# A two-layer hybrid decoder step: VectorE, ScalarE and GpSimd in program order

## Chip, cores and metric

One core of one Trainium2 chip. The metric is the device time of one launch in microseconds, as the median of several runs.

## The reference

One inference step of a decoder with two layers, d = 1024, on 544 tokens: a prompt of 512 and 8 samples of 4 tokens, which share the weights. Cut to what matters, per layer:

```
h  = rmsnorm(x) * (1 + scale1(c)) + shift1(c)
z  = h @ W_in                       # all mixers' inputs and the merge gates
A  = causal pooling (windows 2, 4, 8, 16), a linear map per group
B  = retention, 4 heads, rotary q and k, chunks of 128, group norm, swish gate
C  = B_ * conv3(C_ * h_)            # short gated convolution
D  = RWKV-7: token shift, decay, delta-rule state S = S*w + (S a) b + v k, gate
mixed = sum over branches of sigmoid(gate_i) * (branch_i @ W_i)
x  = x + gate1(c) * (mixed @ W_out)
h2 = rmsnorm(x) * (1 + scale2(c)) + shift2(c)
u  = causal_dwconv3(h2 @ W_up);  x = x + gate2(c) * ((silu(u_a) * u_b) @ W_down)
```

After the second layer a final RMSNorm. The new states of every mixer are outputs too. All data is fp32.

## The kernel before

**Matmuls.** Channels lie on the 128 partitions and tokens in the free dimension, in two halves of 272 columns. A product of fp32 accuracy is made of three matmuls (`mm3`: hi of the weight times hi and lo of the input, lo of the weight times hi of the input; L137, L138, L139, and L164, L165, L166 after the change). A weight unit is 128x1024: a DMA on SyncE's queue brings it as `raw` (three buffers), ScalarE makes `whi` by a CAST (L117), VectorE, and in two cases GpSimd, makes `wlo`, the residual (L118). A unit gives 24 matmuls per half into a PSUM bank `pd` (three buffers). Small matmuls go to `pm` (five buffers).

**Main stream and generators.** `tile_hybrid_step` emits the main stream (first steps of the input projection by `first_units` together with the modulation's products, the rest of the projection, `gates` four times, out-projection, FFN up and down, norm), and after every three matmuls it calls `slot()`, which lets generators (`spawn`) go a step if they are due: `rwkv` with its scan, `retentions`, the norms, the modulation's weights. A `yield n` in a generator says after how many matmuls the next step is due. So each piece of side work has its place among the matmuls.

**Who sets the order.** The tile framework schedules. TensorE is under `manual_schedule`: its instructions run in the order in which the program emits them. For the other engines a scheduler with a simulated timeline sets the order (`schedule_with_timeline_sim=True`), and `tc.high_priority()` moves a few evacuations ahead:

```
with tile.TileContext(nc, schedule_with_timeline_sim=True) as tc:
    with tc.manual_schedule(engines={mybir.EngineType.PE}):
```

**Names and lines that come up below.** `evac_rw` evacuates a unit of RWKV's input (ScalarE L1008 copy, L1009 scaled copy; VectorE L1013 adds the token shift). `products(T)` makes the decays and key products of a chunk (ScalarE L467, L468; VectorE L477, L479, L485, L491), which L510 multiplies. `substitute` solves a triangular system in 31 steps on VectorE and GpSimd, before the scan. The scan (`psG`, `gs` L625, matmul L630) has gaps of D_G, D_S and D_P matmuls between its steps. `gates` makes a sigmoid per unit-half (ScalarE L1140), the branch's product, times the sigmoid (VectorE L1122) and the sum (VectorE or GpSimd L1124). RWKV's last stage is VectorE L782 to L786 and a split into hi (ScalarE L398) and lo (VectorE L399). In `retention`, L803 to L813 are the transposes' copies and masks, L835 to L842 the chunk states (L836, L838 on VectorE, used by the matmul L855), L871 to L877 the outputs' copies and squares, L387 the group norm's matmul with L392 and L395 on ScalarE (a square root, or a logarithm or exponential, each with a table load). `residual` adds a projection to x (VectorE L350, for the samples L354, L357), `sum_sq` squares (ScalarE L280) and adds (VectorE L283), `rstd_of` sums by a matmul (L291), takes a root (L293) and a reciprocal (L294); `norm_half` multiplies (L313), `modulate` scales and shifts (ScalarE L301, samples on VectorE L304, L305), and splits (L398, L399).

Of the kernel before, what the change touches and what calls it, by code (L numbers as in the profile page):

```python
# [25 lines left out]
D_G, D_S, D_P = 16, 16, 20  # L26
# [17 lines left out]
def tile_hybrid_step(ctx: ExitStack, tc: tile.TileContext, io: dict):  # L44
# [63 lines left out]
    def load_unit(l, u):  # L108
        raw = wp.tile([128, 1024], F32, tag="raw", name=nm("raw"), bufs=3)
        nc.sync.dma_start(raw, io["wst"][l, u])  # L110
        dst = extra_pools.get((l, u))
# [5 lines left out]
        S.copy(hi, raw)  # L117
        (G if (l, u) in ((0, 1), (0, 2)) else V).tensor_tensor(out=lo, in0=raw, in1=hi, op=SUB)  # L118
        wloaded[(l, u)] = (hi, lo)

    order = [(l, u) for l in range(L) for u in range(NU)]
    wpos = [0]

    def prefetch(l, u, ahead):
        while wpos[0] < len(order) and wpos[0] <= l * NU + u + ahead:
            load_unit(*order[wpos[0]])
            wpos[0] += 1

    def getw(l, u, ahead=3):
        prefetch(l, u, ahead)  # L130
        return wloaded[(l, u)]
# [16 lines left out]
    nmm, gens = [0], []  # L148
# [15 lines left out]
    def slot():  # L164
        for e in [e for e in gens if not e["pe"] and nmm[0] >= e["due"]]:  # L165
# [111 lines left out]
    def sum_sq(acc, x):  # L277
# [5 lines left out]
        V.tensor_tensor(out=acc, in0=acc, in1=sq, op=ADD)  # L283
        return acc

    def rstd_of(accs):

        out = []
        for acc in accs:
            ps = PM()  # L290
            PE.matmul(ps[:, 0:HALF], lhsT=ones, rhs=acc, start=True, stop=True)  # L291
            rs = ZR(HALF)
            S.activation(rs, ps[:, 0:HALF], AF.Sqrt, bias=EPS6)  # L293
            V.reciprocal(rs, rs)  # L294
            out.append(rs)
        return out

    def modulate(u, k, half, sA, shA, hh):
        c0, c1 = HS[half]
        npc = HALF if half == 0 else SEQ - HALF  # L300
        S.activation(u[:, :npc], u[:, :npc], AF.Identity, bias=shA[:, k, 0:1], scale=sA[:, k, 0:1])  # L301
        if half == 1:
            us = smp(u[:, npc:HALF])
# [93 lines left out]
    def split_hilo(src, hi, lo):  # L397
        S.copy(hi, src)  # L398
        V.tensor_tensor(out=lo, in0=src, in1=hi, op=SUB)  # L399

    def rwkv(l, za, zb, M, yD):
# [51 lines left out]
        def products(T):  # L453
# [41 lines left out]
        bkn = products(0)  # L495
        yield 60, True
        for T in range(5):
# [3 lines left out]
            if T < 4:  # L501
                bkn = products(T + 1)
# [30 lines left out]
            if T < 4:  # L533
                yield 56, True
# [1045 lines left out]
```

## Time and profile before

| | |
|---|---|
| runs | 1990.83, 1991.24, 1987.48 us; median 1990.83 |
| profiled execution | 1989.65 us, its span 1987.9 us |
| mean granted TensorE clock | 0.984 |
| busy: TensorE matmul | 1916.1 us, 96% |
| busy: weight load | 1837.4 us, 92% |
| busy: VectorE | 1099.3 us, 55% |
| busy: ScalarE | 837.2 us, 42% |
| busy: GpSimd | 330.0 us, 17% |

One execution was profiled. PE is TensorE's matmul, PEld its weight load (it overlaps), DVE VectorE, ACT ScalarE, POOL GpSimd, SP SyncE. L12 is line 12 of the kernel. Times are us from the span's start unless marked ns. In a table of stretches each engine has its busy time and count, PEclk is the TensorE clock that the throttle granted (1.00 is full speed). In a list of waits a row names who waited, for whom, the total, the number of waits and the longest. In a timeline a row has its start, its length, the instruction, and in brackets the idle time before it with what ended it.

### The profile page before, as it was taken

Reading aid. Unit: us, or ns where it says so; the run is one execution under the profiler, and the core shown is the slowest. Engines: PE = TensorE matmul, PEld = TensorE weight load, DVE = VectorE, ACT = ScalarE, POOL = GpSimd, SP = SyncE. Lnnn points to the kernel's source line nnn. Section 1 sums busy time; section 2 is a strip of 40 time slices with the busy share of each in tenths; the row PEclk is TensorE's granted clock in tenths of the full one; section 3 lists DMA queues with packets and bytes.
Section 4 is the critical chain, followed back from the end, with each engine's and each line's share of the span. In section 5 each row is a group of like instructions: output and inputs, shape, how many; then the busy total and the mean of one; then the engine's idle time right before and its main releaser. Section 6 shows DMA issues by size and latency. Waiting matters only on the chain.

```text
span 1987.9 us, 39257 instructions
## 1 busy us (share of the span) xinstructions
PE 1916.1 (96%) x16188; PEld 1837.4 (92%) x16188; DVE 1099.3 (55%) x2245; ACT 837.2 (42%) x1585; POOL 330.0 (17%) x655
## 2 busy tenths in 40 slices
PE   5999999999999999999999999999999999999997
PEld 4989998889999998899999899989899999999997
DVE  5476655443565643456673766554435766455565
ACT  4643233263345531435355433334523555243542
POOL 2210024213001210102202101342210012011210
PEclk8999999999999999999999999999999999999999
DMA  8223434512433257622332133233124222222231
GB/s 319 87 86 99 139 118 151 171 58 85 133 114 136 86 205 292 233 86 85 126 123 65 65 86 86 67 122 102 58 88 162 72 75 89 93 86 86 89 100 47
DMA packets 75555, 227.16 MB, mean 114 GB/s; under 512 B 20208, under 2 KB 23072, under 8 KB 73584
## 3 DMA queue, kind: packets, MB, share of 16 engines
q1 hardware_dynamic: 69872, 210.43, 31.7%
q0 software_dynamic: 3536, 11.53, 1.7%
q10 hardware_dynamic: 1968, 2.69, 0.5%
q8 instruction: 127, 2.08, 0.4%
q14 instruction: 52, 0.43, 0.1%
HBM read 213.33 MB, written 9.06 MB: 112 GB/s over the span
## 4 chain that ended last, share of the span: by engine, by line
PE 87%; DVE 5%; ACT 3%; DMA 2%; issue 2%; SPq 0%; ACTq 0%; DVEq 0%; POOL 0%; POOLq 0%
PE pd L137 27%; PE pd L139 26%; PE pd L138 26%; PE pm L240 2%; DVE wlo L118 1%; DMA raw<-in_wst 1%; PE pm L663 1%; PE pm L683 1%; DVE z L617 1%; PE pm L687 1%; DMA t<-in_xinit 0%; DMA t<-in_wada 0%; PE pm L510 0%; DVE t L953 0%; PE pm L517 0%
## 5 line engine op out<-in xcount | busy, mean ns | idle before, releaser
L137 PE MATMUL pd<-t,whi 128*128 128x272 f32 x4104 | 1211.3, 295 | 21.1 <-ACT t L398 9.6
L138 PE MATMUL pd<-t,whi 128*128 128x272 f32 x4104 | 1186.2, 289 | 5.7 <-DVE t L399 5.7
L139 PE MATMUL pd<-t,wlo 128*128 128x272 f32 x4104 | 1191.0, 290 | 0.0
L137 PEld LDWEIGHTS pd<-t,whi 128*128 128x128 f32 x4104 | 777.5, 189 | 56.6 <-issue 23.8
L138 PEld LDWEIGHTS pd<-t,whi 128*128 128x128 f32 x4104 | 779.4, 190 | 7.8 <-DVE t L399 6.5
L139 PEld LDWEIGHTS pd<-t,wlo 128*128 128x128 f32 x4104 | 778.3, 190 | 0.0
L118 DVE TENSOR_TENSOR wlo<-raw,whi 128x1024 fp32r<-128x1024 f32 x256 | 315.3, 1232 | 318.6 <-ACT whi L117 318.0
L117 ACT CAST whi<-raw 128x1024 fp32r<-128x1024 f32 x258 | 270.5, 1049 | 447.0 <-PE pd L138 425.0
L1287 POOL COPY off<-zr 128x18 f32<-128x18 f32 x88 | 77.2, 877 | 572.4 <-ACT zr L1285 572.4
L350 DVE SCALAR_TENSOR_TENSOR t<-pd,mod,t 128x272 f32<-128x272 f32 (+1 forms) x160 | 76.5, 479 | 115.2 <-PE pd L139 115.0
L1285 ACT COPY zr<-pd 128x272 f32<-128x272 f32 (+2 forms) x264 | 72.9, 311 | 85.4 <-PE pd L139 85.4
L1140 ACT ACTIVATE zr<-pd 128x272 f32<-128x272 f32 x128 | 50.6, 396 | 123.4 <-PE pd L139 122.9
L1124 POOL TENSOR_TENSOR t<-t,zr 128x272 f32<-128x272 f32 x64 | 73.6, 1168 | 144.6 <-DVE zr L1122 106.4
L1122 DVE TENSOR_TENSOR zr<-pd,zr 128x272 f32<-128x272 f32 x96 | 40.5, 435 | 90.3 <-PE pd L139 89.9
L1051 DVE SCALAR_TENSOR_TENSOR zr<-zr,par,zr 128x560 f32<-128x560 f32 x92 | 73.4, 801 | 6.6 <-ACT zr L1050 6.6
L1052 DVE SCALAR_TENSOR_TENSOR zr<-zr,par,zr 128x560 f32<-128x560 f32 x92 | 73.6, 801 | 2.7
L1050 ACT ACTIVATE zr<-zr,par 128x560 f32<-128x560 f32 x92 | 70.0, 764 | 7.0
L399 DVE TENSOR_TENSOR t<-zr,t 128x544 fp32r<-128x544 f32 (+1 forms) x96 | 54.2, 578 | 29.2 <-ACT t L398 29.2
L280 ACT ACTIVATE zr<-t 128x272 f32<-128x272 f32 (+1 forms) x72 | 31.9, 454 | 88.4 <-DVE t L350 62.1
L398 ACT CAST t<-zr 128x544 fp32r<-128x544 f32 (+1 forms) x96 | 48.8, 530 | 47.7 <-DVE zr L1298 46.7
L139 PE MATMUL pd<-t,t 128*128 128x272 f32 x224 | 64.7, 289 | 0.0
L137 PE MATMUL pd<-t,t 128*128 128x272 f32 x224 | 64.5, 288 | 0.0
(283 smaller groups left out, 1777.4 us busy)
## 6 DMA issues: line engine op xcount, KB each, us to landing
raw<-in_wst SPq DMA_DIRECT2D x276, 512.0 KB, 3.4
t<-in_wada SPq DMA_DIRECT2D x32, 1024.0 KB, 9.2
raw<-in_wada SPq DMA_DIRECT2D x24, 512.0 KB, 3.5
zr<-in_rope POOLq DMA_DIRECT2D x16, 272.0 KB, 3.8
t<-in_wada SPq DMA_DIRECT2D x8, 512.0 KB, 6.9
t<-in_xT SPq DMA_DIRECT2D x4, 544.0 KB, 6.4
zr<-zr ACTq DMA_DIRECT2D x32, 68.0 KB, 3.2
t<-in_xT SPq DMA_DIRECT2D x2, 1088.0 KB, 8.5
```

The source lines that it names most:

```text
L117: S.copy(hi, raw)
L118: (G if (l, u) in ((0, 1), (0, 2)) else V).tensor_tensor(out=lo, in0=raw, in1=hi, op=SUB)
L137: PE.matmul(ps, lhsT=a, rhs=xh, start=first, stop=False)
L138: PE.matmul(ps, lhsT=a, rhs=xl, start=False, stop=False)
L139: PE.matmul(ps, lhsT=b, rhs=xh, start=False, stop=last)
L350: V.scalar_tensor_tensor(out=x[:, c0:c0 + npc], in0=ps[:, :npc], scalar=gate[:, m, 0:1], in1=x[:, c0:c0 + npc], op0=MUL, op1=ADD)
L1050: S.activation(cv, u[:, 0:560], AF.Copy, scale=wcol(0))
L1051: V.scalar_tensor_tensor(out=cv, in0=u[:, 1:561], scalar=wcol(1), in1=cv, op0=MUL, op1=ADD)
L1052: V.scalar_tensor_tensor(out=cv, in0=u[:, 2:562], scalar=wcol(2), in1=cv, op0=MUL, op1=ADD)
L1124: (V if last else G).tensor_tensor(out=a[:, c0:c1], in0=a[:, c0:c1], in1=gs, op=ADD)
L1285: pad_evac(lambda o, i, sl: S.copy(o, i), u, ps, half, 2)
L1287: G.tensor_copy(off[:, 22 * s + j], u[:, 512:562].rearrange("p (x t) -> p x t", t=2)[:, 0:25:3, :])
```

## The change

All four of TensorE, VectorE, ScalarE and GpSimd run in program order, without the simulated timeline; SyncE's queue alone is still scheduled. For this the program is written so that what depends on another engine is emitted some matmuls later: `later(n, fn)` holds back an operation until n more matmuls have been emitted, `flush` emits what is held. Weights are loaded in another way: four units are held at most, and when a unit is done the next is loaded (`done`, `fill`). The pieces of the norm, of `products` and of the FFN's convolution are spread over the matmuls. The gaps of the scan get shorter, those of the substitution longer. The same instructions run: 2247 of VectorE, and 7 of ScalarE's table loads fewer, 1615 in place of 1622. The matmuls stand in the same order, but for the mixers' pieces: the substitution is spread over 90 matmuls more, the scan over 96 fewer.

```diff
-D_G, D_S, D_P = 16, 16, 20
+D_G, D_S, D_P = 14, 14, 18
...
+    def load_next(n=10):
+        if not raw_q:
+            load_raw()
+        l, u, raw = raw_q.pop(0)
+        wpos[0] += 1
...
+            held.add((l, u))
         S.copy(hi, raw)
-        (G if (l, u) in ((0, 1), (0, 2)) else V).tensor_tensor(out=lo, in0=raw, in1=hi, op=SUB)
+        def sub():
+            if subs.pop((l, u), None):
+                (G if (l, u) in ((0, 1), (0, 2)) else V).tensor_tensor(out=lo, in0=raw, in1=hi, op=SUB)
+        subs[(l, u)] = sub
+        later(n, sub)
...
+    def fill():
+        while wpos[0] < len(order):
+            x = order[wpos[0]] in extra_pools
+            if not x and len(held) == 4:
+                break
+            load_next()
+            if x:
+                break
+    def done(l, u):
+        held.discard((l, u))
+        fill()
-    def getw(l, u, ahead=3):
-        prefetch(l, u, ahead)
+    def getw(l, u):
+        while (l, u) not in wloaded:
+            load_next()
+        if (l, u) in subs:
+            subs[(l, u)]()
         return wloaded[(l, u)]
...
+    def later(n, fn):
+        laters.append((nmm[0] + n, fn))
...
     def slot():
+        flush(False)
...
-        V.tensor_tensor(out=acc, in0=acc, in1=sq, op=ADD)
+        later(5, lambda: V.tensor_tensor(out=acc, in0=acc, in1=sq, op=ADD))
...
     def norm_half(xt, half, acc, sA, shA, hh):
-        rs = rstd_of([acc])[0]
-        for k in range(8):
-            u = ZR(HALF)
-            V.tensor_tensor(out=u, in0=xk(xt, k)[:, c0:c1], in1=rs, op=MUL)
-            modulate(u, k, half, sA, shA, hh)
-            yield -6
+        rs = rstd_sqrt(acc)
+        yield -8
+        V.reciprocal(rs, rs)
+        yield -10
+        us = {}
+        for i in range(11):
+            if i < 8:
+                us[i] = ZR(HALF)
+                V.tensor_tensor(out=us[i], in0=xk(xt, i)[:, c0:c1], in1=rs, op=MUL)
+            if 0 <= i - 1 < 8:
+                mod_samples(us[i - 1], i - 1, half, sA, shA)
+                mod_prompt(us[i - 1], i - 1, half, sA, shA)
+            if 0 <= i - 2 < 8:
+                S.copy(hilo_of(i - 2, half, hh)[0], us[i - 2])
+            if 0 <= i - 3:
+                hi, lo = hilo_of(i - 3, half, hh)
+                V.tensor_tensor(out=lo, in0=us[i - 3], in1=hi, op=SUB)
+            yield -11 if half == 0 else -7
...
-    def split_hilo(src, hi, lo):
+    def split_hilo(src, hi, lo, n=6):
         S.copy(hi, src)
-        V.tensor_tensor(out=lo, in0=src, in1=hi, op=SUB)
+        later(n, lambda: V.tensor_tensor(out=lo, in0=src, in1=hi, op=SUB))
...
-        bkn = products(0)
-        yield 60, True
+        e1 = decays(0)
+        yield -16
+        bkn = products(0, e1)
+        yield 44, True
...
             if s % 2:
-                yield -14, False, s > 28
+                yield -20, False, s > 28
...
             for half in range(2):
                 for i in range(3):
                     evac_rw(i, ps0[half][i], half)
+            for i in range(3):
+                done(l, i)
...
                     if last:
-                        split_hilo(a[:, c0:c1], mix[m // 4][:, m % 4, c0:c1], mix[2 + m // 4][:, m % 4, c0:c1])
+                        later(4, lambda a=a[:, c0:c1], hl=hilo_of(m, half, mix): split_hilo(a, *hl))
...
-                G.tensor_tensor(out=qs, in0=qs, in1=tb[1], op=MUL)
-                V.tensor_tensor(out=rt[:, kind, :], in0=qn, in1=qs, op=ADD)
+                later(20, lambda qs=qs, t=tb[1]: G.tensor_tensor(out=qs, in0=qs, in1=t, op=MUL))
+                later(36, lambda o=rt[:, kind, :], qn=qn, qs=qs: V.tensor_tensor(out=o, in0=qn, in1=qs, op=ADD))
...
-    with tile.TileContext(nc, schedule_with_timeline_sim=True) as tc:
-        with tc.manual_schedule(engines={mybir.EngineType.PE}):
+    with tile.TileContext(nc) as tc:
+        with tc.manual_schedule(engines={getattr(mybir.EngineType, e) for e in ("PE", "DVE", "Activation", "Pool")}):
```

What this moves shows at three places. First ScalarE behind the first eight steps of the input projection in layer 0, where six banks (`pd_`, `pm_`) are evacuated and weights (`whi_`) are cast. Before:

```order
L1008 COPY zr_631<-pd_192 128x272
L1009 ACTIVATE t_72_615<-pd_192,omm_601 128x272
L117 CAST whi_652<-raw_650 128x1024
L1008 COPY zr_623<-pm_193 128x272
L1009 ACTIVATE t_72_615<-pm_193,omm_601 128x272
L117 CAST whi_658<-raw_656 128x1024
```

And after, with the fourth unit's weight as whi_643 (before, that CAST, of whi_619, stood 32 rows ahead of the one of whi_652):

```order
L1099 COPY zr_621<-pm_182 128x272
L1100 ACTIVATE t_72_615<-pm_182,omm_601 128x272
L1099 COPY zr_625<-pm_183 128x272
L1100 ACTIVATE t_72_615<-pm_183,omm_601 128x272
L130 CAST whi_643<-raw_641 128x1024
L130 CAST whi_648<-raw_646 128x1024
```

The CASTs moved from among the six pairs of evacuations to behind them all.

Second, ScalarE where RWKV's last stage and retention's first part run beside the gates in layer 0 (`t_656` and `t_651` are RWKV's split, `t_632` and `t_630` retention's outputs). Before:

```order
L1140 ACT_TABLE_LOAD
L1140 ACTIVATE zr_4821<-pd_4735 128x272
L398 CAST t_656_4802<-t_73_616 128x544
L871 COPY t_632_4686<-pm_4836 128x512
L839 ACTIVATE t_632_4686<-t_632_4686,cst 128x64
L872 COPY t_632_4686<-pm_4851 128x32
L398 CAST t_656_4802<-t_73_616 128x544
L875 ACTIVATE zr_4877<-t_632_4686 128x544
```

After, where L910 is the old L839, L942 to L946 the old L871 to L875, and L456 the old L398:

```order
L910 ACTIVATE t_630_4659<-t_630_4659,cst 128x64
L456 CAST t_651_4769<-t_73_616 128x544 x2
L1247 ACT_TABLE_LOAD
L1247 ACTIVATE zr_4788<-pd_4702 128x272
L130 CAST whi_4792<-raw_4790 128x1024
L942 COPY t_630_4659<-pm_4809 128x512
L943 COPY t_630_4659<-pm_4824 128x32
L946 ACTIVATE zr_4850<-t_630_4659 128x544
```

The two CASTs now stand ahead of the sigmoid's table load, and all of it with a weight's CAST ahead of retention's copies.

Third, VectorE at the end of layer 0, where the second half's last residuals of x (`t_835`, `t_841`) and the first half's norm meet. Before:

```order
L350 SCALAR_TENSOR_TENSOR t_835_6212<-pd_11667,mod_97,t_835_6212 128x240
L354 TENSOR_TENSOR zs_11687<-pd_11667,mod_97 128x32
L283 TENSOR_TENSOR zr_11464<-zr_11464,zr_11586 128x272
L118 TENSOR_TENSOR t_1522_11738<-raw_11736,t_1522_11738 128x1024
L357 TENSOR_TENSOR t_835_6212<-t_835_6212,zs_11661 128x32
L399 TENSOR_TENSOR t_1433_11223<-zr_11560,t_1431_11221 128x272
L399 TENSOR_TENSOR t_1433_11223<-zr_11571,t_1431_11221 128x272
L357 TENSOR_TENSOR t_835_6212<-t_835_6212,zs_11687 128x32
L283 TENSOR_TENSOR zr_11464<-zr_11464,zr_11612 128x272
L283 TENSOR_TENSOR zr_11464<-zr_11464,zr_11638 128x272
L283 TENSOR_TENSOR zr_11464<-zr_11464,zr_11664 128x272
L283 TENSOR_TENSOR zr_11464<-zr_11464,zr_11690 128x272
```

After, with L408, L412 and L415 for the old L350, L354 and L357, L369 for L399, L325 for L283:

```order
L369 TENSOR_TENSOR t_1436_11229<-zr_11592,t_1434_11227 128x272
L325 TENSOR_TENSOR zr_11446<-zr_11446,zr_11659 128x272
L369 TENSOR_TENSOR t_1436_11229<-zr_11610,t_1434_11227 128x272
L408 SCALAR_TENSOR_TENSOR t_841_6224<-pd_11661,mod_97,t_841_6224 128x240
L412 TENSOR_TENSOR zs_11690<-pd_11661,mod_97 128x32
L415 TENSOR_TENSOR t_841_6224<-t_841_6224,zs_11690 128x32
L325 TENSOR_TENSOR zr_11446<-zr_11446,zr_11693 128x272
L369 TENSOR_TENSOR t_1436_11229<-zr_11640,t_1434_11227 128x272
L369 TENSOR_TENSOR t_1436_11229<-zr_11665,t_1434_11227 128x272
```

The four additions of squares that stood at the end are spread, two residuals of the norm's split are last, and the weights' residuals L118 (L134) no longer stand among them.

More of the change, by code (lines that the diff above doesn't have):

```diff
@@ L451, in rwkv, with decays @@
         dec = M["dec"]
-        def products(T):
+        def decays(T):
             n = 128 if T < 4 else 32
@@ L501, in rwkv @@
             if T < 4:
-                bkn = products(T + 1)
+                e1 = decays(T + 1)
             psA = PM()
@@ L930, in tile_hybrid_step @@
         raw_first(k)
-    prefetch(0, 0, 2)
+    for k in range(3):
+        load_raw()
     sbs = T4(w=(2176,))
@@ L942, in tile_hybrid_step, with normed @@
     ps0 = [[PD() for _ in range(3)], [PM() for _ in range(3)]]
+    xh0 = [[xk(xt, k)[:, c0:c1] for c0, c1 in HS] for k in range(8)]
+    def normed(k):
+        for x, rs in zip(xh0[k], rss):
+            V.tensor_tensor(out=x, in0=x, in1=rs, op=MUL)
+    normed(0)
     for k in range(8):
@@ L1027, in tile_hybrid_step @@
                 extra_pools[(l, i)] = extra_t4
-            ws = [getw(l, u, 0) for u in range(6)]
             for half in range(2):
                 for i in range(6):
-                    evac_rw(i, unit(ws[i], 0, hops, half), half)
+                    evac_rw(i, unit(getw(l, i), 0, hops, half), half)
+                    if half:
+                        done(l, i)
+                    else:
+                        fill()
                 finish(ng)
@@ L1037, in tile_hybrid_step @@
                 evac_rw(i, unit(w, 0, hops, half), half)
+            done(l, i)
+        flush()
         ui = 8
@@ L1186, in tile_hybrid_step @@
                 V.tensor_tensor(out=mm[r, 0:15], in0=mm[r, 0:15], in1=u[r, 15:30], op=SUB)
+            for q in range(2):
+                later(6 + 8 * len(adds) + 8 * q, lambda q=q, f=means: f(q))
             mms.append(mm)
@@ L1253, in tile_hybrid_step @@
         hh = new_hh()
-        ws = [getw(l, ui + m, 0) for m in range(8)]
-        ui += 8
+        o0, ui = ui, ui + 8
         def run_out(m, half):
-            x = residual(xt, m, unit(ws[m], 0, mops, half), half, mod[:, 16:24, :])
+            x = residual(xt, m, unit(getw(l, o0 + m), 0, mops, half), half, mod[:, 16:24, :])
             if half == 1:
-                prefetch(l, ui + m // 2, -1)
+                done(l, o0 + m)
             return x
@@ L1306, in up_pairs @@
             if first:
-                ws = [getw(l, ui + i, 0) for i in range(2 * len(js))]
                 for half in range(2):
@@ L1337, in run @@
                     ti = m * K + k
-                    w = getw(l, base_u + ti // 8, 3)
+                    w = getw(l, base_u + ti // 8)
                     xh, xl = aops[k]
                     mm3(ps[:, :HALF], w, ti % 8, (xh[:, c0:c1], xl[:, c0:c1]), k == 0, k == K - 1)
-                return residual(xt, m, ps, half, mod[:, 40:48, :])
+                x = residual(xt, m, ps, half, mod[:, 40:48, :])
+                if half == 1:
+                    for i in range(m * K // 8, (m + 1) * K // 8):
+                        done(l, base_u + i)
+                return x
             if part == 3:
```

180 lines of the change are left out of this document (113 added, 67 removed).

## The prediction

> **What bounds the kernel now.** I read the page first, its busy times, then its costliest groups.
>
> ```profile
> span 1987.9 us, 39257 instructions
> PE 1916.1 (96%) x16188; PEld 1837.4 (92%) x16188; DVE 1099.3 (55%) x2245; ACT 837.2 (42%) x1585; POOL 330.0 (17%) x655
> ...
> L118 DVE TENSOR_TENSOR wlo<-raw,whi 128x1024 fp32r<-128x1024 f32 x256 | 315.3, 1232 | 318.6 <-ACT whi L117 318.0
> L117 ACT CAST whi<-raw 128x1024 fp32r<-128x1024 f32 x258 | 270.5, 1049 | 447.0 <-PE pd L138 425.0
> ```
>
> TensorE is busy for 1916.1 of 1987.9 us; VectorE and ScalarE are half idle. Both kernels issue the same matmuls, so the change can only move the 71.8 us in which TensorE stands still, and the time in which its clock is halved. The table of stretches says where those are:
>
> ```profile
> core 0: us, PE busy (x) PEld busy (x) DVE busy (x) ACT busy (x) POOL busy (x), PEclk, DMA share, GB/s
> 0.00:50.00 50.00, 26.39 (x325) 22.96 (x326) 29.01 (x65) 23.54 (x45) 11.37 (x29) 0.83 0.82 318
> 50.00:100.00 50.00, 50.00 (x411) 48.77 (x412) 19.87 (x30) 29.92 (x64) 10.77 (x20) 1.00 0.27 86
> 100.00:150.00 50.00, 46.21 (x493) 42.82 (x492) 35.53 (x76) 22.57 (x38) 7.19 (x17) 0.97 0.27 86
> 400.00:450.00 50.00, 45.24 (x434) 39.70 (x433) 23.35 (x46) 34.39 (x50) 6.93 (x10) 0.93 0.15 50
> 1000.00:1050.00 50.00, 46.50 (x346) 45.30 (x345) 35.27 (x96) 29.49 (x63) 1.34 (x9) 0.93 0.33 109
> 1500.00:1550.00 50.00, 47.82 (x362) 46.88 (x362) 26.85 (x50) 16.83 (x31) 0.00 (x0) 0.97 0.45 151
> 1950.00:1987.90 37.90, 26.27 (x204) 25.39 (x202) 22.31 (x57) 7.33 (x15) 0.00 (x0) 0.89 0.18 59
> ```
>
> The first 50 us idle for 23.6 and the last 38 for 11.6, which leaves 71.8 - 35.2 = 36.6 us in the middle. There a granted clock under 1.00 stands wherever TensorE had stood still; a stretch at 0.93 lost 7% of 50 = 3.5 us, one at 0.97 lost 1.5 us, on top of its idle time. The waits of TensorE name what it stood for:
>
> ```profile
> PE pm L291 <- DVE zr L283: 15.6, 3, 12.8
> PE pd L137 <- ACT t L398: 9.6, 2, 9.1
> PE pm L510 <- DVE zr L491: 7.6, 2, 3.8
> PE pd L137 <- DVE zr L1122: 6.3, 6, 1.9
> PE pd L138 <- DVE t L399: 5.7, 3, 2.6
> PE pd L137 <- DVE t L1122: 4.7, 5, 1.6
> PE pm L855 <- DVE t L838: 4.9, 4, 1.7
> PE pm L630 <- DVE gs L625: 4.5, 6, 2.6
> ```
>
> Total, times, longest. Apart from the start (the 12.8 and the 9.1), each is an operation of VectorE that came late by 1 to 4 us. So this is a change of some 36 us of idle and some 15 of clock, spread over about 25 places; 4.0 us (0.2%) is about what a measurement of this kernel can tell from no change.
>
> **The first in-projection units: a new wait.** Before, ScalarE mixes evacuations with CASTs, and the next unit's weights are there when the eight first steps end.
>
> ```profile
> 59.50 0.39 ACT L1008 COPY zr<-pd 128x272 f32<-128x272 f32 x1 [0.76 <-PE pd L139]
> 59.79 0.50 ACT L1009 ACTIVATE t<-pd,omm 128x272 f32<-128x272 f32 x1
> 60.17 0.39 ACT L1008 COPY zr<-pd 128x272 f32<-128x272 f32 x1
> ...
> 61.46 1.09 ACT L117 CAST whi<-raw 128x1024 fp32r<-128x1024 f32 x1
> ```
>
> And TensorE there:
>
> ```profile
> 61.19 0.29 PE L137 MATMUL pd<-t,whi 128*128 128x272 f32 x1
> 61.31 0.29 PE L138 MATMUL pd<-t,whi 128*128 128x272 f32 x1
> ```
>
> At 61.19 the fourth unit starts with no wait. After the change nothing loads it ahead: it is loaded by `done`, which the program reaches behind six evacuation pairs, and ScalarE now keeps that order. A pair takes 60.17 - 59.50 = 0.67 us, so six end at 59.50 + 4.0 = 63.5, the CAST (1.09) at 64.6, and the residual on VectorE (1.23, L118 above; `getw` orders it at once) at 65.8. TensorE, ready at 61.19, needs whi for its first two matmuls and wlo for its third: it comes out 65.8 - 61.2 - 0.25 = 4.3 us late, 3.4 + 0.9 as two waits. Waits of this length are followed by a lowered clock elsewhere (3.8 us at L510 stands in the stretch at 0.97, 1.5 us); as it may not come here, I add half of that: **+5** (bounds +3, if evacuations run at the 0.39 pitch of their first half, and +6.5).
>
> On the clock the Trainium skill, "TensorE: Matmul & The Clock Gate", Part 1 (The HAM clock gate), says that the array falls to half rate after about 3.4 us of idleness. By it a wait of 3.4 us is just at the edge and this term would be 4.3 or 5.8. The trace is stricter: the stretch at 1000 to 1050 us, at 0.93, has no single wait over 2.62 us.
>
> **The start.** The first main matmul waited 9.1 us for L398. GpSimd makes two of the first three residuals:
>
> ```profile
> 21.24 6.50 POOL L118 TENSOR_TENSOR wlo<-raw,whi 128x1024 fp32r<-128x1024 f32 x2 [6.11 <-ACT whi L117]
> ```
>
> They ended at 27.7. After, ScalarE casts those two weights only behind the first norm step's operations, about 4.7 us later, so they end near 32.4, and the first step's matmuls, which ended at 36.6, can end some 2.5 us behind that. What follows of the start's 23.6 us of idle is paced by the modulation's weights; on SyncE's queue these no longer stand behind weights that wait for GpSimd's residuals. I take **-1** (-2 to +1).
>
> **decays/products before the scan (L510 <- L491).** 7.6 us in two waits, one per layer, and 1.5 us of clock each. After: the two Exps are 16 matmuls (2 us at the 0.12 pitch of 61.19 and 61.31) ahead of the products and one pair of table loads is gone, but kkb's products and the conv's additions now stand ahead of them in VectorE's queue for about the same time: **0** (-5 to +2).
>
> **Substitution beside the gates (L1122, t).** A step of the triangular solve every 20 matmuls (2.5 us) in place of 14 (1.75): the gates' L1122 finds VectorE free. 4.7 us of waits fall to about 2; with one lowered clock stretch fewer **-3.5** (-6 to +1). The 90 matmuls by which the solve ends later are taken from the scan's gaps of 16, 16, 20 that become 14, 14, 18.
>
> **The scan (L630 <- gs).** 4.5 us, of which one wait of 2.6 stood behind a rope addition that itself waited for GpSimd. In the new order the addition comes 36 matmuls behind, 4.5 us after its GpSimd product is asked for at 20: that 2.6 goes. Gaps two matmuls shorter take 0.25 us of slack from each of 24 steps that have had about 1 us: **-2.5** (-4 to +4).
>
> **Retention and the tail of RWKV.** Here the order costs.
>
> ```profile
> 411.73 1.28 ACT L1140 ACT_TABLE_LOAD   x1
> 413.03 0.40 ACT L1140 ACTIVATE zr<-pd 128x272 f32<-128x272 f32 x1
> 414.38 0.65 ACT L398 CAST t<-t 128x544 fp32r<-128x544 f32 x1 [0.96 <-DVE t L786]
> 415.02 0.59 ACT L871 COPY t<-pm 128x512 f32<-128x512 f32 x1
> ...
> 417.10 0.65 ACT L875 ACTIVATE zr<-t 128x544 f32<-128x544 f32 x1
> ...
> 413.16 0.55 DVE L783 TENSOR_SCALAR t<-t,par 128x544 f32<-128x544 f32 x1
> 413.63 0.72 DVE L786 TENSOR_TENSOR t<-t,t 128x544 f32<-128x544 f32 x1
> ...
> 413.30 0.43 PE L855 MATMUL pm<-t,t 64*64 64x128 f32 x4 [1.68 <-DVE t L838]
> ```
>
> Before, VectorE takes retention's L838 between the eight operations of RWKV's last stage (L782 to L786), and L855 waits 4.9 us in all; ScalarE lets the table load and the sigmoid go ahead of the CAST that waits for VectorE. After, L909 (the old L838) stands ahead of those eight, so this wait goes. But ScalarE takes both CASTs L456 first: eight operations of 0.55 to 0.72 (5.2 us), a CAST 0.65, table load 1.28, sigmoid 0.40, weight CAST 1.05, then the copies L942 and L943 (0.59 by L871, and a small one) and L946 (0.65 by L875), which releases the matmul L445: 10 us. TensorE covers only about half (12 + 24 main matmuls at 0.12 and some 34 small ones): a wait of about 4 us, and behind it a second chain of the same sort (L955, CAST, table, sigmoid, CAST, the copies L874), about 2.5. So per layer 6.5 us and some 2.5 of clock; before, L855 (4.9) and the two waits of 1.9 in L1122 zr give 8.7 in both layers together; the clock lost 3.5 in the first layer's stretch at 0.93, and I count 1.5 for its second wait and as much again for the second layer, 10: 18.7. After: 18. The terms nearly cancel; I take **+1** (-5 to +7).
>
> **Out-projection and layer boundaries.** Before, VectorE does things at L399 in an order that leaves the last residuals late:
>
> ```profile
> 1028.72 0.39 PE L137 MATMUL pd<-t,whi 128*128 128x272 f32 x1
> 1031.73 0.59 PE L138 MATMUL pd<-t,whi 128*128 128x272 f32 x1 [2.62 <-DVE t L399]
> ...
> 1034.11 1.27 PE L291 MATMUL pm<-zr,cst 128*128 128x272 f32 x2 [0.88 <-DVE zr L283]
> ```
>
> and VectorE's operations there, by line, mean ns behind the busy time:
>
> ```profile
> L350 DVE SCALAR_TENSOR_TENSOR t<-pd,mod,t 128x240 f32<-128x240 f32 (+1 forms) x10 | 4.6, 459 | 2.3 <-PE pd L139 2.3
> L283 DVE TENSOR_TENSOR zr<-zr,zr 128x272 f32<-128x272 f32 x9 | 3.9, 436 | 1.3 <-ACT zr L280 1.1
> ```
>
> The layer boundary loses 2.62 + 0.88 and about 0.6 beside them, and 3.5 in clock: 7.6. After, the squares' additions no longer pile up at the end and the weights of the next layer's first four units are already cast; but the last two residuals L369 stand behind the last residual of x (L408, 0.46 by L350), its two small operations, a square and an addition (L325, 0.44 by L283), so about 2 us of wait and 1 of clock stay: **-4.5** (-7.5 to 0). The two boundaries from gates to the out-projection lose the rest of L399, 5.7 - 2.6 = 3.1, with 0.8 of other lines, and 1.5 in clock at 1500 to 1550: 5.4. After, the split stands 4 matmuls behind the sum and its residual 6 more, and the weight loads come one at a time: about 1 stays, **-4.5** (-5.5 to 0).
>
> **The rest.** From out-projection to FFN VectorE's work between two releases about equals TensorE's time, +0.5. Places that had no wait get in-order waits that I can't see in any row: bound below by 0, above by the waits of L1122 that the trace has (11.0 us in 11), I take near the low end, **+1.5** (0 to +6). Seven fewer table loads of 1.28 us are ScalarE time beside TensorE: 0. The end (L283, L291, square root, reciprocal, eight products) keeps its chain: 0.
>
> **Sum**: +5 - 1 + 0 - 3.5 - 2.5 + 1 - 4.5 - 4.5 + 0.5 + 1.5 = -8 us on a span of 1987.9, so 1980; the profiled execution took 1989.65 with what lies around the span, so 1981.7, and the median of the runs is 1.2 higher than that execution: **1983**.
>
> **Rivals.**
> Slower: gates in a strict order. Each of the 128 sigmoids (L1140) and products (L1122, L1124) gives back a PSUM buffer of a unit; there are three, and a unit-half takes 24 matmuls, 3 us. If the one operation at the head of VectorE's or ScalarE's queue waits longer than the two spare buffers (6 us) less what the gate itself takes, TensorE waits with it. The L1140 row above stood right after a table load; the retention chain of 10 us is over that point. If such heads double the 11.0 us of L1122 waits instead of taking 3.5 off, and lower the clock in three more stretches (4.5): 1983 + 3.5 + 11 + 4.5 = 2002. Against it: in the places I followed, operations are emitted 5 to 36 matmuls behind what they need. Chance 0.22.
> The Trainium skill, "TensorE: Matmul & The Clock Gate", in its paragraph on engine queue depths, says that ScalarE and VectorE run a strict first-in-first-out queue, so a head that waits holds all behind it; the trace agrees (the CAST at 414.38 waits 0.96 and L871 comes only behind it).
> No net change: the boundary gains (9 us) don't come, because VectorE has the same work between the same two matmuls and order alone doesn't shorten it; 1991 + 1 = 1992. For it: VectorE was 70% busy at 1000 to 1050. Chance 0.18.
> More: retention's new waits don't come (ScalarE's copies arrive in time, as L871 did), -14 on those 18, and the first unit's wait is only 3: 1983 - 15 - 2 = 1966. Chance 0.15.
> Forecast as summed: 0.45, its own range 1975 to 1989.
>
> **How the numbers follow.** Of the forecast's 0.45 about 0.38 lies under 1986.9 (0.2% below the median), the rest within; the stronger case adds 0.15, and a little of the others 0.05: faster 0.58. Same 0.18, from the third case and edges; slower 0.24. The range 1963 to 2002 leaves out the tails of the two outer cases, 0.1 each.
>
> **What the profile after would show.** A wait of 3 to 4.5 us of L164 on L130 and L134 at about 60 us (if absent, the first term is wrong). Waits of L855's successor (L926) gone, and waits of L445 on L946 of about 4 us per layer instead. Waits on L369 at the layer boundary under 2 us and PEclk there above 0.95. L1122's successors down to 6 to 8 us in all. If TensorE's waits list new rows on gates (L1247's sigmoids) with more than 10 us, the rival that ends slower is right.

## The result and the profile after

The changed kernel takes 2018.37 us (2014.91 to 2021.17, four runs) against 1990.96 before: a ratio of 1.0141, interval 1.0122 to 1.0160. It is slower by 1.4%, where 1983 was forecast. The span of the profiled execution grew from 1987.9 to 2019.4 us.

The page of the changed kernel, and TensorE's list of waits (total, times, longest):

```profile
span 2019.4 us, 39097 instructions
PE 1927.6 (95%) x16188; PEld 1847.3 (91%) x16188; DVE 1098.5 (54%) x2245; ACT 807.6 (40%) x1578; POOL 236.8 (12%) x655
```

```profile
PE pm L331 <- DVE zr L325: 15.7, 2, 12.5
PE pd L164 <- DVE t L408: 9.3, 4, 2.4
PE pm L734 <- DVE z L767: 9.2, 4, 2.9
PE pm L800 <- POOL z L796: 7.4, 2, 4.5
PE pm L445 <- ACT zr L946: 6.1, 2, 3.1
PE pd L164 <- DVE zr L1227: 4.5, 12, 0.9
PE pm L579 <- DVE zr L558: 4.1, 2, 2.0
PE pd L165 <- DVE t L369: 3.9, 3, 1.9
PE pd L164 <- ACT whi L130: 3.2, 1, 3.2
PE pm L896 <- ACT t L874: 3.1, 2, 1.6
```

VectorE and GpSimd run as many instructions as before; GpSimd is even less busy (236.8 us against 330.0). The waits have changed places. Behind the start's two, L510, L1122, L399, L855 and L630 stood at the head of the list before; now L1227 (the old L1122) is down from 11.0 to 4.5 and L579 (the old L510) from 7.6 to 4.1, and new rows stand above them: L734 and L800, the first matmul of a scan step (for the prompt and for the samples), and L164 behind L408, in FFN's down-projection.

Idle time and clock show in the same places. The table of stretches, in the columns of the one before:

```profile
50.00:100.00 50.00, 45.92 (x365) 45.05 (x364) 20.61 (x31) 25.81 (x52) 5.30 (x25) 0.93 0.27 86
350.00:400.00 50.00, 43.43 (x417) 40.50 (x417) 21.81 (x55) 12.53 (x37) 16.09 (x28) 0.90 0.44 141
950.00:1000.00 50.00, 47.57 (x367) 47.36 (x366) 30.17 (x52) 20.20 (x38) 9.13 (x27) 0.97 0.35 113
1000.00:1050.00 50.00, 46.79 (x366) 45.73 (x364) 32.56 (x74) 20.10 (x36) 0.10 (x1) 1.00 0.29 102
1050.00:1100.00 50.00, 47.90 (x351) 46.99 (x352) 27.07 (x57) 26.69 (x59) 3.29 (x21) 0.93 0.28 97
```

350 to 400 us, in layer 0's scan, lost 6.6 us idle and 10% of the clock, 5 us.

To see where the time goes I took the start of the n-th main matmul in both traces (those of L137 to L139, now L164 to L166; they are the same and in the same order) and subtracted. A step in the difference is time lost or won in that part, or time of the mixers' small matmuls that moved into it or out of it.

| part (main matmuls) | after minus before, us |
|---|---|
| start and first units (to 200) | +5.2 |
| layer 0: to the scan's start (200 to 1300) | -6.9 |
| layer 0: scan, then retention's matmuls (1300 to 2300) | +19.5 |
| layer 0: gates behind them (2300 to 2500) | -4.1 |
| layer 0: gates, out-projection, FFN up (2500 to 5100) | -2.2 |
| layer 0: rest of FFN (5100 to 6600) | +7.0 |
| layer boundary (6600 to 7000) | +2.9 |
| layer 1: to the scan's start (7000 to 7800) | -6.9 |
| layer 1: scan, then retention's matmuls (7800 to 8900) | +15.8 |
| layer 1: gates behind them (8900 to 9100) | -5.5 |
| layer 1: gates to the end | +5.2 |
| sum | +30.0 |

The two rows of the scan are +35, but this is not all the scan's loss. They also hold retention's waits (L445 and L896, at main matmuls 2196, 2238, 8820 and 8862), and small matmuls have moved into them from the rows around them: 68 in layer 0 and 82 in layer 1. Idle time and clock don't count such moves. The stretch of the scan that ends ahead of retention's waits, from main matmul 1300 to 2172 and in layer 1 from 7800 to 8796, before:

```profile
249.15:406.53 157.38, 155.84 (x1469) 141.92 (x1467) 78.69 (x200) 54.16 (x132) 49.85 (x88) 1.00 0.44 144
1215.97:1387.32 171.35, 166.99 (x1520) 158.62 (x1518) 96.68 (x237) 60.97 (x151) 54.16 (x99) 1.00 0.29 92
```

and after:

```profile
247.40:426.90 179.50, 168.11 (x1601) 151.32 (x1599) 89.02 (x238) 57.18 (x146) 55.54 (x97) 0.97 0.40 130
1230.49:1416.75 186.26, 176.67 (x1602) 166.43 (x1600) 102.15 (x270) 62.21 (x158) 60.93 (x112) 0.97 0.29 89
```

Before, TensorE stood still for 1.5 + 4.4 = 5.9 us at full clock; after, for 11.4 + 9.6 = 21.0 us, and the clock of 0.97 takes 5.4 + 5.6 us more: 32 in all. So the scans lost 26 us by the change.

What stands at the head of VectorE's queue (the instruction that is next in order) in the scan (start, length, instruction, in brackets the idle time before it and what ended it):

```profile
339.48 0.72 DVE L1339 TENSOR_TENSOR zr<-zr,zr 128x544 f32<-128x544 f32 x1 [4.60 <-DMA zr<-zr]
340.24 0.61 DVE L767 TENSOR_TENSOR z<-pm,pt 64x128 f32<-64x128 f32 x2
...
350.86 0.73 DVE L1339 TENSOR_TENSOR zr<-zr,zr 128x544 f32<-128x544 f32 x1 [5.78 <-DMA zr<-zr]
351.62 0.61 DVE L767 TENSOR_TENSOR z<-pm,pt 64x128 f32<-64x128 f32 x2
```

and on ScalarE and TensorE:

```profile
333.52 2.52 ACTq L1338 DMA_DIRECT2D zr<-zr  x4
```

```profile
340.58 0.81 PE L734 MATMUL pm<-z,t 128*128 128x128 f32 x4 [2.63 <-DVE z L767]
```

L1339 is the rope's `qn *= cos`. It writes over `qn`, from which four DMAs on ScalarE's queue (L1338) are copying the swapped halves, so it must wait until they have landed: they are issued from 333.5 on, the wait ends at 339.5. For 4.6 us VectorE is idle with the scan's L767 right behind, whose PSUM input was finished at 334.6; L767 then goes at once, and TensorE, which needs its `z`, comes out 2.6 us late. In VectorE's own list of waits the whole kernel has this:

```profile
DVE zr L1339 <- DMA zr<-zr: 36.5, 8, 5.9
```

Before, VectorE was idle for these DMAs ahead of the same instruction (L1230) for only 5.9 us, in 4 of its 8 executions: the scheduler had put operations of the scan between the DMAs and it (L696 at 338.94, L1230 right behind it at 339.58). GpSimd is held by the same DMAs at L1340, `qs *= sin`, which reads what they bring and is emitted 20 matmuls behind them:

```profile
390.66 1.88 POOL L1340 TENSOR_TENSOR zr<-zr,zr 128x544 f32<-128x544 f32 x1 [7.23 <-DMA zr<-zr]
392.49 0.57 POOL L793 DMA_DIRECT2D o_wkv_p<-pn  x1
393.06 0.48 POOL L796 MEMSET z<- 64x128 f32 x2
```

and L800 waits 4.52 us for the memset L796.

### The profile page after: what moved, and what is told of

It is laid out like the page before. It is cut to its first block, busy times and chain, and to the rows that moved or that the text cites. A ratio compares the mean times of both kernels' runs of the same rounds, so it can differ in the third digit from the quotient of the medians.

```text
span 2019.4 us, 39097 instructions
## 1 busy us (share of the span) xinstructions
PE 1927.6 (95%) x16188; PEld 1847.3 (91%) x16188; DVE 1098.5 (54%) x2245; ACT 807.6 (40%) x1578; POOL 236.8 (12%) x655
## 5 line engine op out<-in xcount | busy, mean ns | idle before, releaser
L164 PE MATMUL pd<-t,whi 128*128 128x272 f32 x4104 | 1212.5, 295 | 20.8 <-DVE t L408 9.3
L166 PE MATMUL pd<-t,wlo 128*128 128x272 f32 x4104 | 1194.6, 291 | 4.6 <-POOL wlo L134 2.4
L164 PEld LDWEIGHTS pd<-t,whi 128*128 128x128 f32 x4104 | 780.4, 190 | 55.1 <-issue 22.6
L166 PEld LDWEIGHTS pd<-t,wlo 128*128 128x128 f32 x4104 | 780.7, 190 | 5.8 <-POOL wlo L134 3.1
L134 DVE TENSOR_TENSOR wlo<-raw,whi 128x1024 fp32r<-128x1024 f32 x256 | 321.6, 1257 | 125.6 <-ACT whi L130 123.4
L1247 ACT ACTIVATE zr<-pd 128x272 f32<-128x272 f32 x128 | 50.7, 397 | 225.1 <-PE pd L166 213.9
L408 DVE SCALAR_TENSOR_TENSOR t<-pd,mod,t 128x272 f32<-128x272 f32 (+1 forms) x160 | 76.4, 481 | 92.3 <-PE pd L166 92.2
L1397 POOL COPY off<-zr 128x18 f32<-128x18 f32 x88 | 25.8, 293 | 646.7 <-ACT zr L1395 646.7
L1227 DVE TENSOR_TENSOR zr<-pd,zr 128x272 f32<-128x272 f32 x96 | 40.7, 436 | 84.3 <-PE pd L166 83.8
L456 ACT CAST t<-zr 128x544 fp32r<-128x544 f32 x48 | 31.1, 648 | 108.2 <-DVE zr L1413 108.1
L1229 POOL TENSOR_TENSOR t<-t,zr 128x272 f32<-128x272 f32 x64 | 57.9, 920 | 112.1 <-DVE zr L1227 106.5
L1148 ACT ACTIVATE zr<-zr,par 128x560 f32<-128x560 f32 x92 | 65.8, 767 | 8.8 <-DVE zr L1177 8.8
L164 PE MATMUL pd<-t,t 128*128 128x272 f32 x224 | 64.8, 289 | 1.7 <-DVE zs L412 1.7
L166 PE MATMUL pd<-t,t 128*128 128x272 f32 x224 | 64.6, 288 | 0.0
L165 PE MATMUL pd<-t,t 128*128 128x272 f32 x224 | 64.4, 288 | 0.0
```

The lines of the kernel that those rows point to most:

```text
L164: PE.matmul(ps, lhsT=a, rhs=xh, start=first, stop=False)
L165: PE.matmul(ps, lhsT=a, rhs=xl, start=False, stop=False)
L166: PE.matmul(ps, lhsT=b, rhs=xh, start=False, stop=last)
L408: V.scalar_tensor_tensor(out=x[:, c0:c0 + npc], in0=ps[:, :npc], scalar=gate[:, m, 0:1], in1=x[:, c0:c0 + npc], op0=MUL, op1=ADD)
L1148: S.activation(cv, u[:, 0:560], AF.Copy, scale=wcol(0))
L1229: (V if last else G).tensor_tensor(out=a[:, c0:c1], in0=a[:, c0:c1], in1=gs, op=ADD)
```

## The experiments

All times are medians; the kernel before took 1991.3, 1991.9 and 1992.9 us beside the three groups of four, and each ratio is to it.

**e1_rope**: the rope behind its DMAs.

```
-                V.tensor_tensor(out=qn, in0=qn, in1=tb[0], op=MUL)
-                later(20, lambda qs=qs, t=tb[1]: G.tensor_tensor(out=qs, in0=qs, in1=t, op=MUL))
-                later(36, lambda o=rt[:, kind, :], qn=qn, qs=qs: V.tensor_tensor(out=o, in0=qn, in1=qs, op=ADD))
+                later(50, lambda qn=qn, t=tb[0]: V.tensor_tensor(out=qn, in0=qn, in1=t, op=MUL))
+                later(50, lambda qs=qs, t=tb[1]: G.tensor_tensor(out=qs, in0=qs, in1=t, op=MUL))
+                later(66, lambda o=rt[:, kind, :], qn=qn, qs=qs: V.tensor_tensor(out=o, in0=qn, in1=qs, op=ADD))
```

> The changed kernel with one edit: the rope's first multiplication on VectorE (L1339) and the one on GpSimd (L1340) are emitted 50 matmuls after the swap's DMAs are issued, the addition 66, in place of 0, 20 and 36. Theory A (L1339 at the head of VectorE's queue waits for the swap's DMAs and holds the scan's L767 behind it): the waits of L734 on L767 and L769 and of L800 on L796, 18.4 us in the changed kernel, fall under 5, the clock in that part returns to 1.00, and the time falls by 18 to 28 us to 1990 to 2000. Theory B (the scan's gaps of 14, 14 and 18 are too short): under 5 us of change, the waits of L734 stay.

Measured 1992.4, ratio 1.0005 (0.9992 to 1.0018): 26 us of the change's 27 are gone, as expected. The two rows of the table that hold the scan go from +19.5 to +3.5 and from +15.8 to +5.6. The waits of L734 on L767 and of L800 have left the list, and the stretches of the scan are whole again:

```profile
300.00:350.00 50.00, 49.66 (x473) 45.22 (x471) 25.55 (x76) 16.02 (x44) 20.25 (x38) 1.00 0.50 161
350.00:400.00 50.00, 50.00 (x491) 45.37 (x488) 26.04 (x57) 16.50 (x41) 15.27 (x26) 1.00 0.55 178
```

And the scan, in the stretches between the same main matmuls as above, stands still for 1.3 + 4.7 = 6.0 us at full clock, where it was 5.9 before the change:

```profile
245.54:410.54 165.00, 163.67 (x1600) 147.55 (x1598) 87.79 (x238) 57.29 (x146) 52.94 (x97) 1.00 0.44 141
1212.84:1389.65 176.81, 172.13 (x1602) 162.00 (x1600) 103.75 (x270) 62.33 (x158) 58.53 (x112) 1.00 0.31 94
```

**e10_vmul**: VectorE's two operations alone held back, GpSimd's still at 20.

```
-                V.tensor_tensor(out=qn, in0=qn, in1=tb[0], op=MUL)
+                later(50, lambda qn=qn, t=tb[0]: V.tensor_tensor(out=qn, in0=qn, in1=t, op=MUL))
...
-                later(36, lambda o=rt[:, kind, :], qn=qn, qs=qs: V.tensor_tensor(out=o, in0=qn, in1=qs, op=ADD))
+                later(66, lambda o=rt[:, kind, :], qn=qn, qs=qs: V.tensor_tensor(out=o, in0=qn, in1=qs, op=ADD))
```

> The changed kernel with only the rope's VectorE operations held back (L1339 50, L1341 66 matmuls); GpSimd's L1340 stays at 20. Splits the 26 us of e1: the waits of L734 on L767 (9.2 us) are VectorE's head and go; if the waits of L800 on L796 (7.4 us) are GpSimd's head, L1340 waiting for the same DMAs, they stay and with them a lowered clock after the 4.5 us wait: about 2002 to 2008. If L796 was only late because VectorE had been, it is 1992 like e1.

Measured 2001.6, ratio 1.0042 (1.0025 to 1.0060). Its list keeps one of the two rows:

```profile
PE pm L800 <- POOL z L796: 6.8, 2, 3.9
```

So of the 26 us VectorE's head is about 17; the other 9 go when GpSimd's operation is held back too. No run held back GpSimd's alone.

**e2_gaps** and **e7_ropegaps**: is it the scan's shorter gaps? `D_G, D_S, D_P` back to 16, 16, 20, in the changed kernel and in e1_rope.

```
-D_G, D_S, D_P = 14, 14, 18
+D_G, D_S, D_P = 16, 16, 20
```

> The changed kernel with the scan's gaps D_G, D_S, D_P set back from 14, 14, 18 to 16, 16, 20, all else as changed. Theory A: L1339 still stands ahead of L767 and waits the same time for the same DMAs, while a scan step comes 6 matmuls (0.75 us) later: at most 4 us faster, no less than 2010. Theory B: the waits of L734 and L800 go, 15 us or more faster.

> The changed kernel with the rope 50 matmuls behind its DMAs, and the scan's gaps set back to 16, 16, 20. If shorter gaps are a cost once the rope is out of the way, this is faster than 1992.4 by 1 to 4 us; if the gaps only matter in how they meet the rope, it is within 2 us of it; if the shorter gaps are a gain in themselves (fewer matmuls to spread the scan over), it is slower by 2 to 10 us.

2038.8 (ratio 1.0237, 1.0215 to 1.0258) and 2015.6 (1.0120, 1.0105 to 1.0135): 20 and 23 us slower than with the short gaps, where neither text expected more than 10. The rival is refuted, and more than that: the short gaps are worth some 20 us in this program. Yet in e2_gaps the waits of L734 on L767 and of L800 are gone, and these stand in their place:

```profile
PE pm L701 <- DVE gs L696: 14.9, 4, 5.8
PE pm L754 <- DVE z L705: 9.8, 4, 4.9
```

L1339 still waits for its DMAs (7.84 us idle ahead of it at 333.63), and another operation of the scan, L696, now stands behind it. The gaps also differ by more than the constants say: `slot` runs after every three matmuls, so a step takes 48 main matmuls with the short gaps (from 1275 to 1995 L734 comes in 15 steps) and 57 with the long ones (1275 to 2130 in e7_ropegaps), 9 apart and not 6. Over a scan this is 135 matmuls; the 96 given for the change is 16 steps of 6. Against e1_rope, e7_ropegaps falls behind from 1 us at main matmul 1300 to 11 at 2500, and in layer 1 from 12 at 7800 to 22 at 9100: 10 us per layer. Some 7 us of these show as idle time and lowered clock (in layer 0, between 300 and 500 us, 10.2 + 3.0 against 6.1 + 0). Where the rest is, and why the longer gaps cost this much, was not settled.

**e8_vfree** and **e9_vonly**: which engine's order costs? The program under the scheduler again, with all but VectorE in program order (the edit below), and with TensorE and VectorE alone in it. And **e4_sched**, with TensorE alone.

```
-    with tile.TileContext(nc) as tc:
+    with tile.TileContext(nc, schedule_with_timeline_sim=True) as tc:
-        with tc.manual_schedule(engines={getattr(mybir.EngineType, e) for e in ("PE", "DVE", "Activation", "Pool")}):
+        with tc.manual_schedule(engines={getattr(mybir.EngineType, e) for e in ("PE", "Activation", "Pool")}):
```

> The changed kernel's program with the order of the kernel before: only TensorE in program order, the other engines by the scheduler with its simulated timeline. If the order of the other engines is what costs (theory A and the places in the FFN where residuals L408 come behind the convolution), the time falls to 1980 to 1998. If the program's new shape costs (shorter gaps, loads of four units at most, pieces spread), it stays above 2008.

> The changed program with TensorE, ScalarE and GpSimd in program order, and VectorE alone left to the scheduler with its simulated timeline. Theory A and C (the costs stand at the head of VectorE's queue): most of the 36 us between the changed kernel and its program under the scheduler come back, 1983 to 1995. Rival (ScalarE's order costs as much): above 2003.

> The changed program with TensorE and VectorE in program order, ScalarE and GpSimd left to the scheduler: the other side of e8. Theory A and C put the cost at the head of VectorE's queue: the waits on L767 and L408 stay, 2005 to 2020. If instead the two orders have to come together to cost something (VectorE's wait is short when ScalarE may issue the swap's DMAs earlier), it falls under 2000.

| in program order | us | ratio to before |
|---|---|---|
| TensorE (e4_sched) | 1982.6 | 0.9951 (0.9934 to 0.9968) |
| TensorE, ScalarE, GpSimd (e8_vfree) | 1985.2 | 0.9965 (0.9953 to 0.9977) |
| TensorE, VectorE (e9_vonly) | 2014.5 | 1.0111 (1.0092 to 1.0130) |
| all four (after) | 2018.4 | 1.0141 (1.0122 to 1.0160) |

VectorE's order makes up nearly the whole cost of 36 us (2018.4 less 1982.6). In e9_vonly

```profile
PE pm L734 <- DVE z L767: 14.7, 6, 4.8
```

is even longer. GpSimd's waits stay in e8_vfree (L800 on L796, 7.0 us), so its 1985 is not all it could be. And the program in its new shape, without the order, is a gain of 0.5% over the kernel before.

**e3_unit4**: the fourth unit loaded early.

```
         if k < 2:
             for _ in range(1 + k):
                 load_next(0)
+        if k == 3:
+            load_next(0)
```

> The changed kernel with the fourth unit's weight loaded, cast and split during the eight first steps (at the fourth), not behind the six evacuation pairs. Theory: the two waits at 59 to 63 us (3.2 us for the CAST L130, 0.7 for the residual L134) go and with them the clock's fall to 0.93 in the stretch of 50 to 100 us (3.5 us): 6 to 8 us faster. Rival: ScalarE or VectorE is the limit there anyway and the wait moves to the fifth unit: under 2 us.

Measured 2015.2, ratio 1.0108 (1.0080 to 1.0135), an interval that overlaps that of the changed kernel, and less than the 6 to 8 us expected. The trace is clearer than the times. Changed kernel:

```profile
62.66 0.39 PE L164 MATMUL pd<-t,whi 128*128 128x272 f32 x1 [3.25 <-ACT whi L130]
63.92 0.59 PE L166 MATMUL pd<-t,wlo 128*128 128x272 f32 x1 [0.74 <-DVE wlo L134]
```

Both waits are gone in e3_unit4, its stretch of 50 to 100 us has 49.91 us busy at a clock of 1.00, and main matmul 200 comes at -0.3 where it was +5.2. So the place is worth 5.5 us in these two executions, 3 in the medians.

**e5_conv**: the convolution behind the residual that frees a PSUM bank. In the changed kernel, at the start of layer 0's third down-projection:

```profile
983.29 0.80 DVE L1151 SCALAR_TENSOR_TENSOR zr<-zr,par,zr 128x560 f32<-128x560 f32 x1
984.12 0.80 DVE L1152 SCALAR_TENSOR_TENSOR zr<-zr,par,zr 128x560 f32<-128x560 f32 x1
984.84 1.22 DVE L134 TENSOR_TENSOR wlo<-raw,whi 128x1024 fp32r<-128x1024 f32 x1
985.97 0.87 DVE L408 SCALAR_TENSOR_TENSOR t<-pd,mod,t 128x272 f32<-128x272 f32 x2
```

In the second and third of the four down-projections of a layer an output of one half takes only 12 matmuls; L408 empties its bank, and it waits for operations of the FFN pair before. The edit gives the pairs 13 and 21 the offsets 16, 40, 46 and 60 in place of 5, 5, 22 and 30:

```
-        def conv3(u, wcol):
+        def conv3(u, wcol, n=5):
...
-            later(5, rest)
+            later(n, rest)
...
+            n = (16, 40, 46, 60) if j in (13, 21) else (5, 5, 22, 30)
...
-                cvs.append(conv3(upads.pop((j, s)), lambda t, wc=wc: par[:, wc + t:wc + t + 1]))
+                cvs.append(conv3(upads.pop((j, s)), lambda t, wc=wc: par[:, wc + t:wc + t + 1], n[s]))
...
-            later(22, lambda: S.activation(cvs[0], cvs[0], AF.Silu))
+            later(n[2], lambda: S.activation(cvs[0], cvs[0], AF.Silu))
...
-            later(30, product)
+            later(n[3], product)
```

> The changed kernel, with the convolution of the last FFN pair ahead of two of the down-projections (pairs 13 and 21) held back: its two halves come 16 and 40 matmuls after the pair, the product 60, so that the first residuals L408 stand ahead of them in VectorE's queue. Theory C (L408, which frees a PSUM bank after 12 matmuls, waits behind L1151 and L1152, 3.2 us): the four waits of L164 on L408, 9.3 us in all, go, and with them two stretches at 0.97: 8 to 12 us faster, about 2008. Rival: VectorE is late there because the weight's CAST holds ScalarE, and the wait stays or moves to L457: under 3 us.

Measured 2005.1, ratio 1.0065 (1.0050 to 1.0080): 13 us faster. The waits were 9.3 us, and the stretches at 950 and 1800 us go from a clock of 0.97 to 1.00, 1.5 us each. L408 has left the list, and the stretch is full:

```profile
950.00:1000.00 50.00, 49.97 (x398) 49.75 (x398) 32.45 (x59) 19.50 (x36) 7.57 (x24) 1.00 0.36 115
```

**e6_all**: e1_rope, e3_unit4 and e5_conv together, all four engines in program order.

> The changed kernel in program order with three edits: rope 50 matmuls behind its DMAs, the fourth unit loaded early, the convolution held back ahead of the down-projections. If the three places are separate, their gains add: 26 measured, 3 measured, and 8 to 12 expected, from 2018 to 1977 to 1982, faster than the kernel before by 0.4 to 0.7%. If they share one cover, it stays near 1990.

Measured 1976.05, ratio 0.9914 (0.9898 to 0.9931). The gains add: 26 + 3 + 13 from 2018.4 gives 1976.

**e12_sched**: the same program under the scheduler.

> e6_all's program with only TensorE in program order, the others left to the scheduler. If program order gains something of its own once no head of a queue waits long, this is slower than 1976, as the changed program under the scheduler was (1982.6): 1979 to 1986. If the whole gain is the program's new shape, it is within 2 us of 1976 or faster.

Measured 1983.7, ratio 0.9949 (0.9930 to 0.9968). By the medians program order is ahead by about 0.35% once these heads no longer wait long; but the two intervals meet (e6_all ends at 0.9931), and one of the eight times under the scheduler, 1973.5, is below all of e6_all's. So that it is no slower is shown; a gain is likely, not certain. In this kernel's list the waits that the change had taken away are back:

```profile
PE pm L579 <- DVE zr L558: 10.4, 2, 5.2
PE pd L164 <- ACT t L1041: 9.4, 1, 9.4
PE pm L926 <- DVE t L909: 4.9, 4, 1.9
```

**e11_split**: e6_all with RWKV's last split emitted later, so that the sigmoid and retention's copies stand ahead of it on ScalarE.

```
-            split_hilo(y, yD[0][:, 2 * p, :], yD[0][:, 2 * p + 1, :])
+            later(36, lambda y=y, p=p: split_hilo(y, yD[0][:, 2 * p, :], yD[0][:, 2 * p + 1, :]))
```

> e6_all with one more edit: RWKV's last split (the CASTs L456 and residuals L457) is emitted 36 matmuls behind its product, so that on ScalarE the table load, the sigmoid, the weight's CAST and retention's copies stand ahead of it. If the two CASTs that wait for VectorE's eight operations are what holds L946, the waits of L445 on L946 (6.1 us in e6) fall under 3 us and the lowered clock behind them goes: 4 to 9 us faster, about 1969. If retention's second chain takes the time over, within 2 us of 1976.

Measured 1969.79, ratio 0.9890 (0.9872 to 0.9907), the fastest kernel here. The waits of L445, 6.1 us, are gone; the second chain behind them has grown:

```profile
PE pm L896 <- ACT t L874: 5.1, 2, 2.6
```

It was 1.6 us in one wait in e6_all, so the place itself gives 2.6 us of idle time; the clock there is 0.97 in both (400 to 450 us). By the ratios e11_split is 0.24% ahead of e6_all, some 5 us; where the rest comes from was not settled.

## Why the prediction was wrong

**The scan's term failed.** It was -2.5 with bounds -4 and +4; by idle time and clock the two scans lost 26 us, and e1_rope takes 26 back. The step that failed is the account of what the rope costs the scan. It took the addition alone, 36 matmuls behind, and concluded "that 2.6 goes". That wait did go (TensorE's list has no L701 behind L696 any more), though its reason was read wrong: VectorE shows no idle time ahead of that addition, it had worked from 1320.84 to 1328.52 without a break. But I passed over the one line of the rope that the diff leaves as it was, the first multiplication, emitted right behind its DMAs, and so put its wait at nothing; and I took GpSimd's product, 20 matmuls behind, to find its DMAs landed. Under the scheduler the first line cost little; in program order it holds VectorE's queue, for 36.5 us in 8 waits. The trace of before could have priced it. Its operations L1230 and L1231 have these rows of what ended the idle time before them:

```profile
  DMA zr<-zr: 5.9, 4
```

```profile
  DMA zr<-zr: 29.3, 7
```

29.3 us in 7 waits of GpSimd say that the swap takes long to land, and the page of before lists the same DMAs with a median of 3.2 us from issue to landing. That L1230 writes what these DMAs read was in the code.

**The slower rival had the right form and the wrong place.** It said that a head of VectorE's queue which waits longer than the cover holds TensorE, priced on the gates (L1140, L1122), at 2002. The gates' waits fell (11.0 to 4.5, and L1247, the old L1140, has 0.8 us in the list); the heads that held TensorE up were the rope's in the scan and the convolution's in the FFN. That ScalarE's and VectorE's queues are first in, first out (the Trainium skill, "TensorE: Matmul & The Clock Gate", the paragraph on engine queue depths) is what the run shows: L767 starts 0.04 us after L1339 ends (339.48 + 0.72, 340.24).

**The FFN was missing.** I gave +0.5 to the part from out-projection to FFN and nothing to the down-projections. Two of them ask for a bank every 12 matmuls, where an up-projection asks every 24: 9.3 us of waits, 13 us by e5_conv. My unseen in-order waits were put at +1.5, at most +6.

**First units: right.** 3.4 + 0.9 us of waits were forecast, 3.25 + 0.74 measured; +5 and -1 for the start gave +4, the table has +5.2. e3_unit4, without the two waits, has -0.3 in this row, so the waits were worth 5.5 there and the start about nothing.

**Before the scan: right in sign.** L1122 from 11.0 to 4.5; L510, for which I took 0, from 7.6 to 4.1. The parts before the scan gave -6.9 in each layer, of which I had -3.5 for both; some of this is small matmuls that moved behind them into the scan's row. Idle time and lowered clock there fell from about 18 to about 11 us in both layers together.

**Retention: waits and clock put too high.** The wait of L445 on L946 came, 3.0 and 3.1 us against "about 4", and the one at L874 with 1.6 against 2.5. By idle time and clock, from main matmul 2172 to 2500 and from 8796 to 9124, the two layers went from 17.5 to 14 us, where I had 18.7 and 18; the clock took 3.5 of the 14, and I had counted 5. So about -3.5 came in place of +1. e11_split shows that the cause of the first wait was the one named: the two CASTs ahead of the sigmoid.

**Out-projection boundaries: right**, -2.2 in each layer (main matmuls 2500 to 5100 and 9124 to 11724) against -4.5 for both. **Layer boundary: wrong sign.** -4.5 was forecast, about +3 came. The last L369 did wait,

```profile
1050.70 0.39 PE L165 MATMUL pd<-t,whi 128*128 128x272 f32 x1 [1.90 <-DVE t L369]
1053.74 0.60 PE L165 MATMUL pd<-t,whi 128*128 128x272 f32 x1 [1.26 <-DVE t L369]
```

in three waits of 3.9 us in all where I had "about 2", and the clock fell in the stretch from 1050, as it had before. No run took this place alone.

## What to carry to other kernels

When an engine goes from a scheduler's order to program order, each of its instructions that waits for a DMA or another engine becomes a wait for all that the program emits behind it; a scheduler may have put other work ahead of it. So go through the program's emission order and ask of each instruction how long its slowest input, or reader of what it overwrites, takes from issue to landing, and delay it by that many matmuls, also the lines that the change leaves as they are. The list of waits by the waiting engine, in the trace from before, has those times even where TensorE does not wait. Shown here: with three places repaired, program order goes from 1.4% slower than the kernel before to 0.9% faster, and is at least as fast as the scheduler on the same program; a fourth, run in program order alone, gives 1969.8 us, 1.1% under the kernel before.

## What the runs showed of the hardware

Four small DMAs (68 KB each) issued by ScalarE hold ScalarE up as well: 2.52 us of issue, and the CAST behind them began 2.59 us after the engine's last work; from the first issue to the end of VectorE's wait were 6.0 us (333.52 to 339.48). A wait of 2.4 us of TensorE at L408 (986.53 us) stands in a stretch at a clock of 0.97 (950 to 1000 us); another of 2.4 us, at 1948.35, is followed by a stretch at 1.00 (1950 to 2000 us). So such waits lower the clock at some places of an execution and not at others. The Trainium skill ("TensorE: Matmul & The Clock Gate", Part 1) puts the fall at about 3.4 us of idleness, and in the row at 950 us it came at less.
